# A skipped overflow branch moved to the third expert from the end, and one expert's rows turned a unit later

## The chip, the cores and the metric

The kernel runs on one core of a Trainium2 chip. The metric is the device time of one execution in microseconds (us). The engines that matter here are TensorE (PE), VectorE (DVE), ScalarE (ACT), GpSimd (POOL, which issues the gathers and scatters) and SyncE (SP, whose queue issues the loads of the weights).

## The reference, cut to what matters

Two encoder layers run over 512 tokens of width 1024. Each layer has four kinds of attention side by side, an output projection, and then a mixture of 16 experts (4 groups of 4). The change lies in the experts:

```python
def hier_moe(h, wg, bg, we, be, w_gate, w_up, w_down):
    ...
    expert_id = g_idx * EXPERTS_PER_GROUP + e_idx          # one group, two experts of it
    gate = jnp.sum(jax.nn.one_hot(expert_id, N_EXPERTS, dtype=jnp.float32) * (g_w * e_w)[..., None], axis=1)
    y = jnp.zeros_like(t)
    for e in range(N_EXPERTS):
        hid = jax.nn.silu(t @ w_gate[e]) * (t @ w_up[e])
        y = y + gate[:, e:e + 1].astype(t.dtype) * (hid @ w_down[e])
    return y.reshape(b, s, d)
```

All weights are float32. One expert has three matrices of 1024 x 512, 2 MB each.

## The kernel before

**Routing.** For each expert the kernel makes a list of up to `CAP` = 96 tokens that chose it. The rows of these tokens are gathered from DRAM (`gather`, L1477, an indirect DMA on POOL), turned on TensorE (`turn`, L1492) and multiplied with the expert's weights. The result is scaled (L1546, into the buffer `ye`) and added to the output in DRAM (`store`, L1547, an indirect DMA with addition).

**Overflow.** If some expert has more than 96 tokens, `overflow()` treats the rest in further rounds with loops over all experts. The number of rounds is read from `nrd` when the program runs; with these inputs it is 1, and the body below `with tc.If(rounds > 1)` (L1562) is skipped on every engine. The body loads weights with ScalarE's DMAs into the buffer `sg`, splits them into the buffer `ye`, and uses TensorE, DVE and POOL as well. `sg` is the same single buffer into which `silu` (L1511) writes for each expert.

**Precision.** Except for expert 0's gate and up products, which take the weights as loaded (L1504), each product is made of three matmuls on a high and a low part (`mm3`, L299). ScalarE makes the high part of each piece of weights (L155) and DVE the low part (L156). Up to six pieces are split ahead.

**Order.** `MOE_ORDER` interleaves the experts: 0 gate, 0 up, 1 gate, 0 down, 1 up, 2 gate, 1 down, 2 up, and so on to 15 up, 15 down. Each product is cut into four units of 512 KB of weights (a unit takes two of the eight 128-row blocks, or one of the four for down). In each unit the kernel issues TensorE's matmuls, splits further pieces as far as room allows, and does the small work that is tied to this unit: `hidden` (Silu's output times the up product, L1523) and `turn_hidden` (L1532) of the expert before, `turn` of the next expert, and the lists and the gather of a later one (L1465, L372). The order of the program is the order on each engine.

**Loads.** SyncE issues the weights in the same order (L195, L198) into some 26 buffers of 512 KB; a load is issued when a buffer's split is done. The loads run on eight lanes, each with a counter. Behind the expert weights of the first layer follow the weights of the second layer's projections.

**Around the change.** The branch stands behind expert 0's down product. Since its body uses `sg`, Silu of expert 1 cannot keep its place behind expert 1's gate product and is issued after the branch:

```python
                if m == 'g' and e != 1:
                    X[e].silu()
                elif m == 'd' and (last or e < NE - 1):
                    X[e].store()
                if (e, m) == (0, 'd'):

                    overflow()
                    X[1].silu()
```

The second place is `turn` of the next expert (`X[e + 1].turn()`), issued in unit 1 of the up product (units count from 0).

Of the kernel before, what the change touches and what calls it, by code (L numbers as in the profile page):

```python
# [23 lines left out]
NE = 16  # L24
# [33 lines left out]
def _bcast(ap, n=128):  # L58

    return bass.AP(tensor=ap.tensor, offset=ap.offset, ap=[[0, n]] + [list(d) for d in ap.ap])  # L60
# [3 lines left out]
def hybrid_encoder(ctx: ExitStack, tc: tile.TileContext, I: dict, out: bass.AP, depth=2, dbg=None):  # L64
# [289 lines left out]
    for layer in range(depth):  # L354
# [6 lines left out]
        X = {}  # L361
# [7 lines left out]
        def hots(e, oh):  # L369

            for t in range(NT):
                V.tensor_scalar(oh[:, t], iota, pos[:, t, e:e + 1], None, op0=OP.is_equal)  # L372
            return [oh[:, t] for t in range(NT)]
# [13 lines left out]
        with ExitStack() as c2:  # L387
# [475 lines left out]
            with ExitStack() as c3:  # L863
# [431 lines left out]
                g, d = list(range(32, 48)), list(range(48, 56))  # L1295
# [6 lines left out]
                for k, hd in enumerate(heads):  # L1302
                    first, m = place[k * NT], len(hd[2])
# [79 lines left out]
        with ExitStack() as c2:  # L1383
# [221 lines left out]
            def start(e):  # L1605
                rows, X[e] = X[e], Expert(xg[e % 2], X[e])
                if e > 1:
                    X[e].lists(lambda t: parts[:, t, e])
                else:
                    X[e].rows = rows  # L1610
                X[e].gather()
# [3 lines left out]
                          m=lambda: G.memset(xg[1], 0.0), S=lambda: start(1), K=weights,  # L1615
                          q=lambda: G.tensor_copy(parts[..., :2], tokb[:, :, None].to_broadcast([128, NT, NE, 2])))
            tail(TAIL[len(seq) + 5])
            for e, m in MOE_ORDER:
                us = wbase[layer, e, m][0]
                for i, u in enumerate(us):  # L1620
                    W.split(u + 1)
                    end = e == NE - 1 and m != 'g'
                    if m == 'd':
                        X[e].down(i, W.get(u))
                    elif end:
                        X[e].half(i, W.get(u))
                    else:
                        X[e].gu(m, i, W.get(u))
                    W.free(u + 1)
                    if end:  # L1630
                        if m == 'u' and i % 2:
                            X[e].hidden(i // 2)
                        if (m, i) == ('u', 2) or (m, i) == ('d', 0):
                            X[e].turn_hidden(m == 'd')
                    elif m == 'g' and i == 0 and e > 0:
                        X[e - 1].hidden()
                    upto = moe_units[-1] + 1
                    if end and m == 'd' and i > 1:
                        upto += W.RAW
                    W.split(min(u + (AHEAD if end else W.HL), upto), G if (m, i) in GS and not end else V)  # L1640
                    if m == 'g' and i == TH and e > 0:
                        X[e - 1].turn_hidden()
                    if m == 'u' and i == 1 and e + 1 < NE:
                        X[e + 1].turn()

                    for s, todo in FIRST if e < 2 else ((e + 3, (('u', 0), ('u', 2))),):
                        if e > 1:
                            todo = [(e,) + w for w in todo]
                        if (e, m, i) in todo and s < NE:
                            (start if (e, m, i) == todo[1] else listed)(s)  # L1650
                    if m == 'd' and e < 2:
                        if i == 0:
                            X[e].hots = hots(e, sm.tile([128, NT, CAP], BF, name="oh", bufs=2))
                        elif i == 2:
                            X[e].lists(lambda t: parts[:, t, e], rows=e == 0)
                    if m == 'g' and i == 0 and e == NE - 1 and not last:
                        (place, g1), = W.room(1)
                        g1 = g1.bitcast(FT)
                        SP.dma_start(g1, _bcast(I['norm1_g'][layer + 1]))
                    if m == 'u' and i == 0 and e == NE - 1 and not last:  # L1660

                        pt = ps.tile([128, NT, 128], FT, name="pto", tag="tr")
                        for t in range(NT):
                            PE.matmul(pt[:CAP, t], X[e].hots[t], identb, start=True, stop=True)
                        place = place[:, :512].rearrange("p (t c) -> p t c", t=NT)
                        A.activation(place[:CAP], pt[:CAP], AF.Copy)
                        V.tensor_copy(wlast, gate[:, :, NE - 1])
                if m == 'g' and e != 1:
                    X[e].silu()
                elif m == 'd' and (last or e < NE - 1):  # L1670
                    X[e].store()
                if (e, m) == (0, 'd'):

                    overflow()
                    X[1].silu()
                if m == 'd' and e == NE - 2 and not last:

                    for t in range(NT):
                        SP.dma_start(x_sb[:, t], stream[:, t])
# [91 lines left out]
```

## Time and profile before

| | |
|---|---|
| median of 3 runs | 1387.91 us (1387.12 to 1390.14) |
| profiled execution | 1392.77 us |
| its span, first to last instruction | 1391.0 us |
| TensorE busy | 1290.2 us (93%) |
| DVE busy | 1057.1 us (76%) |
| ScalarE busy | 857.8 us (62%) |
| POOL busy | 359.9 us (26%) |
| mean granted TensorE clock | 0.971 of full speed |
| moved by DMA | 278.44 MB, mean 200 GB/s |

The expert loops take about 380 to 700 us (first layer) and 1060 to 1391 us (second layer) of the span. Busy times are sums over stages with different limits; a busy TensorE includes the modelled ends of pipelined matmuls.

### The profile page before, as it was taken

To read this page: it belongs to the slowest core of one execution; us is meant where nothing else is said; L and a number is where in the kernel's file an instruction comes from. 1 tells how busy PE (TensorE), PEld (TensorE's weight loads), DVE (VectorE), ACT (ScalarE), POOL (GpSimd) and SP (SyncE) were. 2 spreads that over 40 slices of the span, in tenths; PEclk is the share of its full clock that TensorE was granted. 3 is DMA by queue.
4 is the path that set the end of the run, shared out by engine and by line. 5 is a ranking of instruction groups with operands and counts; after the bars stand their busy time and mean duration, and the time that the engine had idled before them with its cause. 6 is when DMAs were issued, how large, how long until landed. Compare 5 with 4: busy or idle time off the path is not lost. (4 is left out here: it accounts for less than half of the span.)

```text
span 1391.0 us, 21081 instructions
## 1 busy us (share of the span) xinstructions
PE 1290.2 (93%) x7182; PEld 1003.5 (72%) x7182; DVE 1057.1 (76%) x2073; ACT 857.8 (62%) x1419; POOL 359.9 (26%) x580
## 2 busy tenths in 40 slices
PE   9998899999986999999989998999998699999996
PEld 7776688888844666666778886888885366676674
DVE  5537866878575999999776587586966499999994
ACT  5343366664245888888744545676634378888884
POOL 3105333324411411111041161430344132111120
PEclk9999899999998999999999999999999899999998
DMA  8322341024597999999344223211176899999950
GB/s 230 100 78 63 133 138 41 15 67 168 217 382 264 352 366 362 366 365 329 109 118 125 78 75 79 69 37 31 48 307 239 303 312 358 370 365 366 367 201 13
DMA packets 100575, 278.44 MB, mean 200 GB/s; under 512 B 19466, under 2 KB 30522, under 8 KB 100457
## 3 DMA queue, kind: packets, MB, share of 16 engines
q1 hardware_dynamic: 89816, 249.00, 49.9%
q0 software_dynamic: 10352, 27.41, 7.9%
q8 instruction: 58, 0.95, 0.3%
q10 hardware_dynamic: 288, 0.59, 0.1%
q14 instruction: 61, 0.49, 0.1%
HBM read 264.34 MB, written 24.81 MB: 208 GB/s over the span
## 5 line engine op out<-in xcount | busy, mean ns | idle before, releaser
L156 DVE TENSOR_TENSOR lo<-raw,hi 128x1024 fp32r<-128x1024 f32 (+2 forms) x387 | 463.9, 1221 | 64.2 <-ACT hi L155 56.1
L155 ACT ACTIVATE hi<-raw 128x1024 fp32r<-128x1024 f32 (+1 forms) x393 | 405.4, 1051 | 99.6 <-PE pg L299 28.7
L299 PE MATMUL pm<-lo,hTh 128*128 128x512 f32 (+2 forms) x376 | 132.5, 352 | 5.9 <-DVE lo L156 5.9
L299 PE MATMUL pm<-hi,hTh 128*128 128x512 f32 (+2 forms) x376 | 134.3, 357 | 0.7 <-ACT hTh L155 0.5
L299 PE MATMUL pm<-hi,hTl 128*128 128x512 f32 (+2 forms) x376 | 132.0, 351 | 0.2
L299 PE MATMUL pd<-hi,hl 128*96 128x512 f32 x256 | 102.5, 400 | 4.5 <-DVE hl L156 2.8
L986 PE MATMUL pv<-v,pT 128*128 128x64 f32 x768 | 99.0, 272 | 6.5 <-DVE pT L974 2.7
L299 PE MATMUL pd<-lo,hh 128*96 128x512 f32 x256 | 101.2, 395 | 1.6 <-DVE lo L156 1.6
L986 PEld LDWEIGHTS pv<-v,pT 128*128 128x128 f32 x768 | 94.3, 193 | 10.8 <-DVE pT L974 5.0
L299 PE MATMUL pu<-hi,xh 128*96 128x512 f32 (+1 forms) x256 | 101.1, 395 | 0.6 <-PEq L1562 0.6
L299 PE MATMUL pd<-hi,hh 128*96 128x512 f32 x256 | 101.2, 395 | 0.0
L957 ACT ACTIVATE p<-p,m 128x512 f32<-128x512 f32 x96 | 68.7, 716 | 52.1 <-DVE m L939 51.7
L299 PE MATMUL pu<-hi,xl 128*96 128x512 f32 (+1 forms) x256 | 98.2, 384 | 0.0
L299 PE MATMUL pu<-lo,xh 128*96 128x512 f32 (+1 forms) x256 | 98.2, 384 | 0.0
L299 PE MATMUL pg<-hi,xh 128*96 128x512 f32 x240 | 96.8, 404 | 0.0
L299 PE MATMUL pg<-lo,xh 128*96 128x512 f32 x240 | 95.6, 398 | 0.0
L299 PE MATMUL pg<-hi,xl 128*96 128x512 f32 x240 | 95.3, 397 | 0.0
L299 PEld LDWEIGHTS pm<-lo,hTh 128*128 128x128 f32 x376 | 71.0, 189 | 16.0 <-DVE lo L156 8.0
L299 PEld LDWEIGHTS pm<-hi,hTh 128*128 128x128 f32 x376 | 70.9, 188 | 12.0 <-ACT hTh L155 1.0
L299 PEld LDWEIGHTS pm<-hi,hTl 128*128 128x128 f32 x376 | 71.0, 189 | 9.5 <-DVE hTl L156 0.9
L307 PE MATMUL ptr<-ident,p 128*128 128x128 f32 x512 | 77.3, 273 | 0.3 <-DVE pT L974 0.2
L307 PEld LDWEIGHTS ptr<-ident,p 128*128 128x128 f32 x512 | 63.8, 141 | 17.7 <-DVE pT L974 1.2
(389 smaller groups left out, 2772.5 us busy)
## 6 DMA issues: line engine op xcount, KB each, us to landing
raw<-in_expert_w_down_dram SPq DMA_DIRECT2D x118, 512.0 KB
raw<-in_expert_w_gate_dram SPq DMA_DIRECT2D x114, 512.0 KB
raw<-in_expert_w_up_dram SPq DMA_DIRECT2D x110, 512.0 KB
raw<-in_w_in_dram SPq DMA_DIRECT2D x32, 512.0 KB
raw<-in_w_out_dram SPq DMA_DIRECT2D x16, 512.0 KB
toep<-brep SPq DMA_DIRECT2D x16, 448.0 KB
x_sb<-in_expert_w_gate_dram SPq DMA_DIRECT2D x14, 512.0 KB
x_sb<-in_expert_w_up_dram SPq DMA_DIRECT2D x10, 512.0 KB
```

What stands on the lines that cost most here:

```text
L155: A.activation(hi, src, AF.Copy)
L156: E.tensor_tensor(lo, src, hi.bitcast(FT), op=OP.subtract)
L299: PE.matmul(pt, a, b, start=first and n == 0, stop=last and n == tot - 1)
L307: PE.transpose(pt[:c, i * 128:(i + 1) * 128], s, ident)
L957: A.activation(p, p, AF.Exp, bias=m, scale=-1.0, accum_out=s)
L986: PE.matmul(st['pv'][:, t], self.pT[:, k * 128:(k + 1) * 128], self.v(k), start=k == 0, stop=k == NT - 1)
```

## The change

The branch moves from behind expert 0's down product to behind expert 13's (`NE - 3`), and the Silu that is issued after it is no longer expert 1's but expert 14's (`NE - 2`). In the order of products, expert 14's gate stands before expert 13's down, and 14 up, 15 gate, 14 down, 15 up, 15 down follow. Besides, the rows of expert 1 are turned in unit 2 of expert 0's up product, and no longer in unit 1; for the other experts it stays unit 1.

```diff
-                    if m == 'u' and i == 1 and e + 1 < NE:
+                    if m == 'u' and i == (1 if e else 2) and e + 1 < NE:
                         X[e + 1].turn()
...
-                if m == 'g' and e != 1:
+                if m == 'g' and e != NE - 2:
                     X[e].silu()
                 elif m == 'd' and (last or e < NE - 1):
                     X[e].store()
-                if (e, m) == (0, 'd'):
+                if (e, m) == (NE - 3, 'd'):
 
                     overflow()
-                    X[1].silu()
+                    X[NE - 2].silu()
```

## Rows read from the trace of the kernel before

**Rows 1.** Windows: length, busy time of PE, PEld, DVE, ACT, POOL, PEclk, DMA share, GB/s.
```profile
410.00:424.00 14.00, 10.99 (x56) 7.34 (x54) 7.09 (x16) 5.50 (x7) 2.78 (x2) 1.00 1.03 351
424.00:440.00 16.00, 7.41 (x27) 5.16 (x27) 8.84 (x16) 7.99 (x10) 1.28 (x1) 0.68 0.52 166
...
500.00:520.00 20.00, 19.86 (x97) 13.91 (x96) 18.62 (x25) 16.55 (x20) 2.75 (x2) 1.00 1.01 366
...
1095.00:1112.00 17.00, 5.47 (x28) 3.47 (x26) 2.34 (x6) 3.54 (x5) 1.52 (x1) 0.82 0.65 219
1112.00:1130.00 18.00, 17.25 (x70) 12.00 (x71) 16.49 (x28) 12.42 (x16) 1.25 (x1) 0.79 0.84 275
```

**Rows 2.** Timeline of POOL: the stores of experts 0, 1, 2, then 0, 1.
```profile
417.65 1.52 POOL L1547 DMA_INDIRECT xd<-ye,ix  x1 [4.08 <-ACT ye L1546]
...
449.86 1.47 POOL L1547 DMA_INDIRECT xd<-ye,nrd  x1 [11.27 <-ACT ye L1546]
...
468.15 1.46 POOL L1547 DMA_INDIRECT xd<-ye,ix  x1 [3.40 <-DVE lo L156]
...
1097.15 1.52 POOL L1547 DMA_INDIRECT out_dram<-ye,ix  x1 [4.07 <-ACTq L1562]
...
1131.17 1.45 POOL L1547 DMA_INDIRECT out_dram<-ye,nrd  x1 [12.42 <-ACT ye L1546]
```

**Rows 3.** Timeline of PE: start, length, instruction, idle time before it, releaser.
```profile
432.59 0.78 PE L1465 MATMUL pli<-parts,oh 128*96 128x5 bf16 x4 [11.30 <-DVE oh L372]
...
1112.74 0.78 PE L1465 MATMUL pli<-parts,oh 128*96 128x5 bf16 x4 [11.98 <-DVE oh L372]
```

**Rows 4.** Timeline of ACT: the Silu of expert 1 in both layers.
```profile
429.56 0.59 ACT L1511 ACTIVATE sg<-pg 96x512 f32<-96x512 f32 x1 [12.19 <-SPq L1562]
...
1109.71 0.59 ACT L1511 ACTIVATE sg<-pg 96x512 f32<-96x512 f32 x1 [12.84 <-SPq L1562]
```

**Rows 5.** The line of the branch, 416 to 430 us: ns min/median/max, first and last start.
```profile
L1562 SPq EVENT_SEMAPHORE  x8: 17/17/17, 419.2 to 429.4; - x8
...
L1562 ACTq COMPARE_BRANCH  x1: 50/50/50, 416.7 to 416.7; - x1
...
L1562 POOLq INC_SWDGE_SEM  x1: 732/732/732, 418.2 to 418.2; - x1
...
L1562 ACTq EVENT_SEMAPHORE  x1: 17/17/17, 422.7 to 422.7; - x1
```

**Rows 6.** Waits of the load queue, 470:500, then 580:620: total us, times, longest.
```profile
SPq L198 <- DVE lo L156: 11.7, 12, 1.3
...
SPq L198 <- DMA raw<-in_expert_w_gate_dram: 9.3, 8, 2.1
```

**Rows 7.** Timeline of SP: issues of the last expert loads and the next ones.
```profile
652.28 2.42 SPq L195 DMA_DIRECT2D raw<-in_expert_w_down_dram  x4
673.86 1.51 SPq L195 DMA_DIRECT2D raw<-in_w_in_dram  x2
```

**Rows 8.** DMA in slices of 0.35 us, 655:669, then 1336:1350.
```profile
GB/s 249 228 293 222 275 304 298 334 357 386 398 433 456 398 386 363 316 281 257 199 152 105 94 35 0 0 0 0 0 0 0 0 0 0 0 0 0 0 0 0
...
GB/s 319 313 261 307 278 348 334 357 357 378 439 398 421 351 281 246 234 222 211 140 70 105 70 59 12 0 0 0 0 0 0 0 0 0 0 0 0 0 0 0
```

**Rows 9.** Timeline of ACT: expert 13's output in both layers.
```profile
667.19 1.24 ACT L1546 ACTIVATE ye<-pd,w 96x512 f32<-96x512 f32 x2
...
1348.48 1.24 ACT L1546 ACTIVATE ye<-pd,w 96x512 f32<-96x512 f32 x2
```

**Rows 10.** Timeline of PE around the turn of expert 1's rows.
```profile
388.95 3.60 PE L1504 MATMUL pu<-raw,xh 128*96 128x512 f32 x8
396.49 1.51 PE L1492 MATMUL ptg<-ident,xg 96*128 96x96 f32 x8 [3.94 <-DMA xg<-h2d,nrd]
397.80 6.01 PE L1504 MATMUL pu<-raw,xh 128*96 128x512 f32 x8
...
1076.24 1.51 PE L1492 MATMUL ptg<-ident,xg 96*128 96x96 f32 x8 [4.58 <-DMA xg<-h2d,nrd]
```

## The prediction

> **What bounds the kernel now.** I read the windows first, to see what each stage of the expert loop is limited by. In the steady stretch from 500 to 520 us TensorE is busy 19.86 of 20 us and the DMA engines are full at 366 GB/s: two resources at their limit at once, TensorE ahead by a hair [rows 1]. The stores give the beat: from one store to the next 18.29 us (449.86 to 468.15), which is what an expert costs [rows 2]. In both layers one stretch falls out of this, right behind expert 0: TensorE is busy 7.41 of 16 us from 424 to 440 and 5.47 of 17 us from 1095 to 1112, and there, alone in the loop, the DMA rate falls too, to 166 and 219 GB/s [rows 1].
>
> Then the timelines of TensorE and ScalarE, to see who waits for whom. TensorE stands still for 11.30 and 11.98 us, for a DVE operation that itself waits for work behind ScalarE [rows 3]. ScalarE stands still for 12.19 and 12.84 us in front of one instruction, the Silu of expert 1 (L1511), and what ends that wait is named L1562 on SyncE: the skipped branch [rows 4]. The line of the branch shows why. SyncE runs eight semaphore instructions there, spread from 419.2 to 429.4 us [rows 5]. At that time the load queue holds some eight weight loads of 512 KB; at the steady rate eight of them need 8 x 0.524 MB / 366 GB/s = 11.5 us, the length of the hold. I read this as follows: the branch's body issues loads into the buffer `sg`, so the empty path has to bring each load lane's counter up to date, and that can be done only when the lane's earlier load has landed. The skipped branch drains the load queue, and the Silu that follows writes `sg`.
>
> Last I looked at who waits in the load queue later on. From 470 to 500 us SyncE mainly waits for DVE to free a buffer (the loads are ahead); from 580 to 620 us it waits for earlier loads to land (the loads are the slower stream by then) [rows 6]. The last expert loads of layer 0 are issued from 652.28 to 654.7 us; the next layer's first loads come only at 673.86 [rows 7].
>
> **The change part by part.**
>
> *The early hold goes.* Silu of expert 1 returns to its place behind the gate product, and nothing of 0d waits for SyncE. Between the stores of experts 0 and 1 lie 449.86 - 417.65 = 32.21 us in the first layer and 1131.17 - 1097.15 = 34.02 in the second [rows 2]. Without the hold the same work (one expert) takes the beat of 18.29. Removed: 13.92 + 15.73 = 29.6 us. That is more than ScalarE's two waits (25.0) because TensorE comes out of them at a lower granted clock (0.68 in 424:440, 0.79 in 1112:1130 [rows 1]) and pays for that too. Nothing else is ready to fill that beat with a stall: the loads stand far ahead here, since SyncE waits for free buffers afterwards, not the other way round [rows 6].
>
> *Do the loads keep up?* They win less than the computation. In the hold they lost (366 - 166)/366 x 16 + (366 - 351)/366 x 14 = 9.3 us in layer 0, and 6.8 + 4.5 = 11.3 us in layer 1 (17 us at 219, 18 at 275) [rows 1]. The computation thus eats some 5 to 6 us of their lead per layer. That lead is large for the weights themselves: the last load has landed at about 663.4 us (the 24th slice of 0.35 us is the last that moves anything [rows 8]), when expert 13's output is not yet out (668.4 [rows 9]) and two experts are still to be computed. So the weights never run out, and I put nothing for them.
>
> *The late branch.* It now stands behind expert 13's down product, and Silu of expert 14 behind it. The order of work around it: ScalarE finishes expert 13's output at 667.19 + 1.24 = 668.4 and 1348.48 + 1.24 = 1349.7 us [rows 9]; the queue has run dry by 663.4 and 1336 + 25 x 0.35 = 1344.7 [rows 8]. Today the queue would be empty 5.0 us before ScalarE arrives. After the change ScalarE arrives earlier by 15.7 and 17.5 us (with the next item), the queue is empty earlier by 9.3 and 11.3, so ScalarE arrives 1.4 and 1.2 us too early and is held that long. No further loads stand in front of SyncE: the next layer's come 19 us behind the last expert load, after splits that belong to expert 14 [rows 7]. What is queued behind the Silu on ScalarE: the splits of expert 15's gate weights and rows, then DVE's halves of them, then TensorE. How much a hold costs TensorE can be read from the early one: 12.19 us cost 11.30 of standstill, 12.84 cost 11.98 [rows 3, 4], so hold less 0.9. For 1.3 us that is 0.4, and TensorE's own branch and a late split add a little: I take 1.0 a layer, 2.0 in all. Bounds: nothing (queue empty in time), and 12 us a layer, the early standstill again.
>
> [...] The row first: in layer 0 ScalarE takes the branch at 416.7 us, and its own semaphore instruction behind it comes only at 422.7 [rows 5]; SyncE's counters, later still, hid these 6.0 us. [...]
>
> *Expert 1's rows turned one unit later.* TensorE stands still for 3.94 and 4.58 us in front of these transposes (L1492), until the gather of the rows lands [rows 10]. The unit that now comes first is a quarter of expert 0's up product: four of the eight matmul records that take 3.60 us, so 1.80 us of work that moves into the idle time. The price is cover: the split of the turned rows on ScalarE and DVE, which expert 1's first product needs, then lies beside one unit of TensorE's work (1.8 us) in place of two. I take it as just enough. Gain 1.8 us a layer, 3.6 in all. Lower end 0 (the cover fails by as much); upper end 4.8 a layer, if TensorE, idle for 2.1 in place of 3.9 us, also keeps its clock: the eight records after the wait take 6.01 us in place of 3.60 and the transposes 1.51 in place of about 0.8 [rows 10]. I take the lower clock as it is today, being the nearest row.
>
> Sum against the profiled execution: 1392.8 - 29.6 - 3.6 + 2.0 = 1361.6 us (its span is 1391.0, 1.8 lie around it). The median of the runs is 4.9 below the profiled time, so 1356.7.
>
> **The rivals.**
>
> *The late hold is as real as the early one (0.20).* For it: the same eight lanes, the 6.0 us between ScalarE's branch and its semaphore [rows 5], and the computation arriving before the queue is empty. Against it: a queue that is nearly dry by then [rows 8]. With 4 to 12 us of standstill a layer in place of 1.0 the time is 1363 to 1379.
>
> *The weights bind (0.05).* If the loads' lead were gone, only their own gain of 9.3 + 11.3 = 20.6 us would come out: 1367. Against it: long after the hold SyncE still waits for DVE [rows 6].
>
> *The clock stays up at the early turn (0.12).* Up to 2 x 3.0 us more: 1351.
>
> *The end is later than today (0.04).* The branch also has to bring the store lanes up to date; if that made ScalarE wait for expert 13's scatter behind a full queue, the late hold would be 12.8 us plus the scatter's landing. The change loses from (29.6 + 3.6)/2 = 16.6 us of standstill a layer upward; at 20 it ends at 1388 + 2 x 3.4 = 1395. Against it: POOL's counter instruction in the branch took 0.73 us with a store just issued [rows 5].
>
> *The hold only moves (0.03).* The whole early price of 29.6 us, standstill and slow clock, is paid at the new place: 1388, or 1384 with the turn's 3.6.
>
> **How the numbers follow.** The forecast, 1353 to 1362, has 0.56; the likeliest value is 1357. The clock rival lies below it, the milder half of the late hold and the weights above. From 1349 to 1372 about 0.8 is held. What a measurement of this kernel can tell from no change is about 0.2%, 2.8 us. Faster by more: 0.56 + 0.20 + 0.05 + 0.12 = 0.93; same 0.03; slower 0.04.
>
> **What would show it.** Right: in the changed profile ScalarE has no wait for L1562 near 417 and 1085 us; the first two stores of each layer stand about 18.3 us apart; L1562 appears near 653 us and near 1318; SyncE's eight counters there lie within 3 us; TensorE has no gap over 2 us in the last three experts; and the wait in front of L1492 is about 2.1 and 2.8 us. Wrong: a ScalarE wait of over 5 us at the new place with a TensorE gap behind it, TensorE gaps with weight loads as releaser in experts 8 to 15, or DMA shares under 0.9 in the middle of the loop.

## The result and the profile after

The changed kernel takes 1365.65 us (median of 4 runs, 1364.60 to 1368.58); the kernel before, in the same rounds, takes 1388.89 (4 runs, 1387.12 to 1390.14). The ratio is 0.9837 with an interval of 0.9817 to 0.9857, so it is faster by 23.2 us. The sign and the range (1349 to 1372) hold. The forecast's own case, 1353 to 1362, does not: what came is the first rival, the late hold as real as the early one, though TensorE's standstill was shorter than that rival had it. The profiled execution took 1366.22 us, its span is 1364.1. Of the runs below one stands apart: of the four of the branch behind expert 14 one took 6083 us, for a reason that nothing here shows, and its ratio and the 1351.23 us given there leave it out.

The windows of the kernel after, first in the stretches of [rows 1] and then at the new place (length, busy time of PE, PEld, DVE, ACT, POOL, PEclk, DMA share, GB/s):

```profile
424.00:440.00 16.00, 16.00 (x84) 11.45 (x84) 14.78 (x26) 12.93 (x16) 2.77 (x2) 1.00 1.02 373
500.00:520.00 20.00, 19.86 (x97) 13.88 (x96) 18.56 (x25) 16.55 (x20) 2.74 (x2) 1.00 1.00 359
1095.00:1112.00 17.00, 16.64 (x83) 11.69 (x82) 15.64 (x24) 13.93 (x18) 2.76 (x2) 1.00 1.02 368
1112.00:1130.00 18.00, 17.53 (x87) 12.25 (x86) 16.59 (x23) 14.81 (x18) 3.06 (x2) 1.00 1.02 372
...
656.00:662.00 6.00, 5.06 (x11) 3.01 (x12) 6.00 (x8) 4.79 (x7) 0.00 (x0) 0.50 0.17 42
1325.00:1331.00 6.00, 5.23 (x12) 3.45 (x13) 6.00 (x8) 4.06 (x5) 0.00 (x0) 0.50 0.02 4
```

The hole behind expert 0 is gone in both layers: TensorE is busy 16.00 of 16 us where it was 7.41, at a granted clock of 1.00, and the loads run at 373 GB/s where they ran at 166 [rows 1]. A new one has opened late: in 656:662 and 1325:1331 TensorE is busy for 5.06 and 5.23 of 6 us, but at a granted clock of 0.50.

The stores on POOL's timeline (answering to [rows 2]) give the size of both:

```profile
411.01 1.52 POOL L1547 DMA_INDIRECT xd<-ye,ix  x1 [4.08 <-ACT ye L1546]
429.71 1.47 POOL L1547 DMA_INDIRECT xd<-ye,nrd  x1 [10.56 <-ACT ye L1546]
...
648.29 1.44 POOL L1547 DMA_INDIRECT xd<-ye,ix  x1 [16.19 <-DVEq L1562]
672.54 1.42 POOL L1547 DMA_INDIRECT xd<-ye,ix  x1 [22.81 <-ACT ye L1546]
...
1078.68 1.52 POOL L1547 DMA_INDIRECT out_dram<-ye,ix  x1 [4.07 <-ACT ye L1546]
1097.39 1.45 POOL L1547 DMA_INDIRECT out_dram<-ye,nrd  x1 [10.55 <-ACT ye L1546]
...
1316.42 1.43 POOL L1547 DMA_INDIRECT out_dram<-ye,ix  x1 [16.21 <-DVEq L1562]
1340.86 1.41 POOL L1547 DMA_INDIRECT out_dram<-ye,ix  x1 [23.00 <-ACT ye L1546]
```

From store 0 to store 1 it is now 18.70 and 18.71 us, for 32.21 and 34.02 before. From store 13 to store 14 it is 24.25 and 24.44, for 17.65 in both layers before:

```profile
668.71 1.44 POOL L1547 DMA_INDIRECT xd<-ye,ix  x1 [16.20 <-ACT ye L1546]
686.36 1.42 POOL L1547 DMA_INDIRECT xd<-ye,ix  x1 [16.21 <-ACT ye L1546]
...
1350.00 1.43 POOL L1547 DMA_INDIRECT out_dram<-ye,ix  x1 [16.20 <-ACT ye L1546]
1367.65 1.41 POOL L1547 DMA_INDIRECT out_dram<-ye,ix  x1 [16.22 <-ACT ye L1546]
```

Cut at such marks, the difference of the two spans (1364.1 - 1391.0 = -26.9) adds up:

| stretch | first layer | second layer |
|---|---|---|
| up to the list matmuls ahead of the loop (L1224), or from store 14 of the layer before | -3.5 | -0.5 |
| from there to store 0 | -3.1 | -4.2 |
| store 0 to store 1 | -13.5 | -15.3 |
| store 1 to store 13 | -0.3 | +0.2 |
| store 13 to store 14 | +6.6 | +6.8 |
| store 14 to the end | | -0.1 |

The 3.5 us ahead of the loop lie where nothing was changed; over all traces of this document, none of which changes anything there, these matmuls start anywhere from 373.6 to 379.6 us, and before has the latest. The profiled execution of before was itself 3.9 us above the median of the 4 runs, so the 3.5 are put down to that execution: without them the spans differ by 23.4 us, close to the 23.2 of the medians.

ScalarE's timeline at the new place (answering to [rows 4, 9]):

```profile
646.78 1.24 ACT L1546 ACTIVATE ye<-pd,w 96x512 f32<-96x512 f32 x2
653.66 0.59 ACT L1511 ACTIVATE sg<-pg 96x512 f32<-96x512 f32 x1 [5.65 <-SPq L1562]
...
1314.90 1.24 ACT L1546 ACTIVATE ye<-pd,w 96x512 f32<-96x512 f32 x2
1321.31 0.59 ACT L1511 ACTIVATE sg<-pg 96x512 f32<-96x512 f32 x1 [5.17 <-SPq L1562]
```

The branch's line, 640 to 655 us and then 1308 to 1325 (answering to [rows 5]: ns min/median/max, first and last start):

```profile
L1562 SPq EVENT_SEMAPHORE  x8: 17/17/17, 653.0 to 653.5; - x8
L1562 ACTq COMPARE_BRANCH  x1: 50/50/50, 647.7 to 647.7; - x1
L1562 ACTq EVENT_SEMAPHORE  x1: 17/17/17, 652.1 to 652.1; - x1
...
L1562 SPq EVENT_SEMAPHORE  x8: 17/17/17, 1314.3 to 1321.2; - x8
L1562 ACTq COMPARE_BRANCH  x1: 45/45/45, 1315.7 to 1315.7; - x1
L1562 ACTq EVENT_SEMAPHORE  x1: 17/17/17, 1316.2 to 1316.2; - x1
```

What the reader is to see: in both layers SyncE's last counter (653.5, 1321.2) ends the hold. In the second layer it is the only candidate, because ScalarE's own semaphore instruction comes 0.5 us behind its branch. In the first, ScalarE's own comes 4.4 us behind its branch, and would have held the Silu until 652.1 even without SyncE. Two different delays share the place. That SyncE itself waits for loads, and is not merely late, shows in the packets of the load queue: in the first layer the queue moves its last two in 652:653, just ahead of SyncE's counters, and in the second its last four in 1320:1321, just ahead of the last counter.

TensorE's timeline behind the holds, and around the turn (answering to [rows 3, 10]):

```profile
394.58 0.85 PE L1492 MATMUL ptg<-ident,xg 96*128 96x96 f32 x8 [0.84 <-DMA xg<-h2d,nrd]
395.26 1.88 PE L1504 MATMUL pu<-raw,xh 128*96 128x512 f32 x4
...
656.57 0.74 PE L299 MATMUL pg<-hi,xh 128*96 128x512 f32 x1 [2.84 <-ACT xh L155]
...
1324.22 0.48 PE L299 MATMUL pg<-hi,xh 128*96 128x512 f32 x1 [2.37 <-ACT xh L155]
```

TensorE works on through the first part of each hold and stands still for only 2.84 and 2.37 us, in front of expert 15's gate product, whose rows `xh` are made by ScalarE behind the held Silu. The slow matmuls cost as much again: in that stretch they start 0.43 us apart, ahead of the hold 0.23, and six microseconds at a granted clock of 0.50 are about three lost (an estimate from these numbers).

### The profile page after: what moved, and what is told of

It reads as the page before. It is cut to its first block, busy times and chain, and to the rows that moved or that the text cites. A ratio compares the mean times of both kernels' runs of the same rounds, so it can differ in the third digit from the quotient of the medians.

```text
span 1364.1 us, 21097 instructions
## 1 busy us (share of the span) xinstructions
PE 1286.9 (94%) x7182; PEld 1002.6 (74%) x7182; DVE 1058.3 (78%) x2073; ACT 857.3 (63%) x1419; POOL 337.0 (25%) x580
```

## The experiments

The theory after the result (A): the late hold is the early one over again. It is made by the loads in flight, whose counters the skipped body has to bring up to date, and its length is the distance between ScalarE's arrival and the load queue's running dry. The rival (B): each engine that jumps over the body comes back late by itself, wherever the branch stands, and loads have little to do with it. Every ratio is to the kernel before in the same rounds; the runs fall into four sets of rounds, in which that kernel's median is 1388.89 to 1390.51 us, so medians of different sets compare only roughly. A number in a kernel's name says behind which expert's down product its branch stands; the turn is the second part of the change.

**The branch left out altogether.** This kernel leaves out the overflow rounds. From the kernel after:

```diff
-                if m == 'g' and e != NE - 2:
+                if m == 'g':
...
-                if (e, m) == (NE - 3, 'd'):
-
-                    overflow()
-                    X[NE - 2].silu()
```

> The changed kernel without the overflow rounds at all (that part of the computation is left out), each Silu behind its own gate product. It gives the floor for any place of the branch. From the beats in the changed profile, expert 14's store comes 24.25 and 24.44 us after expert 13's in place of the 17.65 of before: 6.6 + 6.8 = 13.4 us. Theory (the skipped branch drains the load queue, and Silu, which writes the buffer that the branch's body loads into, waits for it): 1365.7 - 13.4 = 1352 us. Rival (the late loss is the end of the loop itself, where loads run out, and not the branch): 1365, with the same gap of 2 to 3 us on TensorE.

1353.36 us, ratio 0.9723 (0.9693 to 0.9753). Store 13 to 14 is 17.67 and 17.65 us, 0 to 1 is 18.72. So the branch at its new place costs some 12 us (12.3 by the medians, 13.4 by the stores), and this is the time that any other placement can be held against.

**The branch one expert later**, behind expert 14's down product, with Silu of expert 15 behind it. From the kernel after:

```diff
-                if m == 'g' and e != NE - 2:
+                if m == 'g' and e != NE - 1:
...
-                if (e, m) == (NE - 3, 'd'):
+                if (e, m) == (NE - 2, 'd'):
 
                     overflow()
-                    X[NE - 2].silu()
+                    X[NE - 1].silu()
```

> The branch one expert later still, behind expert 14's down product, with Silu of expert 15 behind it. Theory (drain): by then the last expert loads have landed, SyncE's eight counters follow each other within 1 us except for the three small first loads of the next layer in layer 0, ScalarE's wait at L1562 is under 1.5 us, and the time is 1352 to 1355. Rival (each taken branch costs ScalarE a fixed hold of some 5 us, for instance to fetch instructions): 5 us holds again and, since less work is left to cover them, 1365 or more.

1351.23 us, ratio 0.9720 (0.9682 to 0.9758): the whole cost is gone, as far as the intervals can tell, with the branch, its loads and its body as they were. The branch's line, first and last start over both layers, and the two Silus behind it:

```profile
L1562 SPq EVENT_SEMAPHORE  x16: 17/17/17, 657.7 to 1313.4; - x16
L1562 ACTq COMPARE_BRANCH  x2: 45/50/54, 662.7 to 1324.8; - x2
L1562 ACTq EVENT_SEMAPHORE  x2: 17/17/17, 663.1 to 1327.7; - x2
```

```profile
663.60 0.59 ACT L1511 ACTIVATE sg<-pg 96x512 f32<-96x512 f32 x1 [0.67 <-DVE wlast L1667]
...
1328.19 0.59 ACT L1511 ACTIVATE sg<-pg 96x512 f32<-96x512 f32 x1 [2.88 <-ACTq L1562]
```

In the second layer SyncE's last counter is through at 1313.4, and ScalarE comes to the branch at 1324.8; in the first the eight end at 659.6, ahead of ScalarE's 662.7. That is A's prediction. But ScalarE's own return took 2.9 us in the second layer, with no load left to wait for: B's delay exists, and here TensorE had no gap over 0.8 us behind it.

**The body's loads into a buffer of their own.** If the Silu waits because the body's loads write `sg`, it should be free when they write another buffer. The buffer is a small one (128 columns), so a block is loaded in four pieces. Edit of the kernel after:

```diff
-                    r = sm.tile([128, 512], FT, name="sg", bufs=1)
-                    A.dma_start(r, w)
                     hl = sm.tile([128, D], FR, name="ye", bufs=1)
-                    split(hl[:, :512], hl[:, 512:], r)
+                    for c in range(0, 512, 128):
+                        r = sm.tile([128, 128], FT, name="ow", bufs=1)
+                        A.dma_start(r, w[:, c:c + 128])
+                        split(hl[:, c:c + 128], hl[:, 512 + c:640 + c], r)
```

> The place of the changed kernel, but the skipped body loads its weights into a small buffer of its own (four loads of 128 columns) and no longer into the buffer that Silu writes. Theory (drain, and Silu held by the shared buffer): SyncE's eight counters still spread over some 5 us, but ScalarE has no wait named L1562 over 1 us, TensorE no gap, 1352 to 1354. Rival (the branch itself holds ScalarE, by fetching or by its own counter): ScalarE still waits 5 us and the time stays at 1365.

1365.83 us, ratio 0.9825 (0.9794 to 0.9855): nothing won, as the rival had it. The wait changed its owner, though:

```profile
653.74 0.59 ACT L1511 ACTIVATE sg<-pg 96x512 f32<-96x512 f32 x1 [4.98 <-DVEq L1563]
```

SyncE no longer ends it. DVE's and ScalarE's own semaphore instructions now come 5.3 and 4.2 us behind their branches (653.6 and 652.7, branches at 648.3 and 648.5), and 5.5 and 4.7 in the second layer. There the Silu starts at 1319.26, ahead of SyncE's last counter at 1319.7; in the first layer SyncE's last comes at 652.9, too near to tell. The edit took one hold away and, by making the body longer (four loads and splits for one), put the other in its place. The same edit with the branch at its old place and the turn kept:

> The branch at its old place behind expert 0's down product, the turn of expert 1's rows as changed, and the body's loads in a buffer of their own. Theory (drain): SyncE still drains the queue for some 11 us and the loads lose 6 to 10 us a layer, but nobody waits for SyncE; the loads' lead covers it, so 1352 to 1355, and then the old place was as good as the new one. Rival (it is the place that counts, since the drain starves the load stream): SyncE's pause is paid in weights that come late in experts 8 to 15, 1370 or more. Rival (the branch itself holds ScalarE): 12 us holds, 1381.

1369.00 us, ratio 0.9834 (0.9797 to 0.9870): neither 1352 to 1355 nor 12 us holds. Nor do weights come late: from store 1 to store 14 the first layer takes 236.5 us, as before the change.

```profile
416.97 0.59 ACT L1511 ACTIVATE sg<-pg 96x512 f32<-96x512 f32 x1 [5.70 <-DVEq L1563]
```

SyncE still counts its lanes off from 419.1 to 428.8 us, and nobody waits for it: the Silu is through at 417, where it stood until 429.56 [rows 4]. So SyncE's hold works through the buffer, as [rows 5] were read; with `sg` out of it the 12 us are gone, and a wait of 5.7 us (TensorE gaps of 3.84 and 3.69) is left, which is B's.

**Each part of the change alone.** The turn without the move, the only edit of the kernel before:

```diff
-                    if m == 'u' and i == 1 and e + 1 < NE:
+                    if m == 'u' and i == (1 if e else 2) and e + 1 < NE:
                         X[e + 1].turn()
```

> The kernel before with only the turn of expert 1's rows one unit later. By the prediction's term 1.8 us a layer, 3.6 in all: 1385 to 1387 against some 1390. From the changed profile (list of expert 0 to store of expert 0: 34.9 and 34.2 us in place of 38.0 and 38.4) 3.1 + 4.2 = 7.3 us: 1381 to 1383. Rival (the turn does nothing for the time): 1389 to 1390.

1391.13 us, ratio 1.0001 (0.9989 to 1.0013): worth nothing. The Silu, and TensorE's gap in both layers:

```profile
428.33 0.59 ACT L1511 ACTIVATE sg<-pg 96x512 f32<-96x512 f32 x1 [17.56 <-SPq L1562]
```

```profile
431.36 0.78 PE L1465 MATMUL pli<-parts,oh 128*96 128x5 bf16 x4 [16.67 <-DVE oh L372]
...
1111.09 0.78 PE L1465 MATMUL pli<-parts,oh 128*96 128x5 bf16 x4 [16.27 <-DVE oh L372]
```

ScalarE gets to the Silu earlier, SyncE's last counter comes at 428.2 as it did at 429.4 [rows 5], and the wait grows from 12.19 to 17.56 us. The loads set the end of the hold, and what the engines win ahead of it becomes waiting.

The move without the turn is the kernel after with that line put back (`i == 1`).

> The changed kernel with the turn put back to unit 1: the branch's move alone. By the beats in the changed profile 13.5 + 15.3 won early and 6.6 + 6.8 lost late: 15.4 us, so 1374 to 1375 against some 1390, and 7 us slower than the changed kernel if the turn is worth what the profile says; 3.6 slower if it is worth the predicted term.

1361.96 us, ratio 0.9802 (0.9783 to 0.9821). The expectation was missed by 12 us: expected 3.6 or 7 us slower than the changed kernel, the move alone is no slower than it. The late Silu and the stores around it:

```profile
651.65 0.59 ACT L1511 ACTIVATE sg<-pg 96x512 f32<-96x512 f32 x1 [2.70 <-PE ptg L1492]
```

```profile
649.22 1.44 POOL L1547 DMA_INDIRECT xd<-ye,ix  x1 [16.20 <-DVEq L1562]
669.76 1.42 POOL L1547 DMA_INDIRECT xd<-ye,ix  x1 [19.10 <-ACT ye L1546]
...
1318.34 1.43 POOL L1547 DMA_INDIRECT out_dram<-ye,ix  x1 [16.21 <-DVEq L1562]
1337.84 1.41 POOL L1547 DMA_INDIRECT out_dram<-ye,ix  x1 [18.08 <-ACT ye L1546]
```

ScalarE's waits are 2.70 and 1.68 us in place of 5.65 and 5.17, the beats 20.54 and 19.50 in place of 24.25 and 24.44. TensorE has no gap over 1.1 us there and keeps a granted clock of 1.00 in 652:664 and 1320:1332. Its turn waited for only 1.71 us in the first layer, where [rows 10] has 3.94, and TensorE kept its clock through that wait (the eight records behind it took 3.60 us). So the wait that the turn was to fill is not of a fixed size. Nor are the 2.70 us the loads' alone: SyncE's last counter comes at 650.6, ScalarE's own semaphore instruction at 651.2, 2.5 us behind its branch. In the second layer SyncE's last, at 1319.6, ends the wait.

**The old place, with nothing to load.** The branch behind expert 0 again, the turn kept, and every load of the body replaced by a memset (so this kernel and the next two leave out the overflow rounds):

```diff
                     r = sm.tile([128, 512], FT, name="sg", bufs=1)
-                    A.dma_start(r, w)
+                    V.memset(r, 0.0)
...
-                    A.dma_start(posd[0].rearrange("(t p) e -> p t e", p=128), pos)
-                    A.dma_start(posd[1].rearrange("(t p) e -> p t e", p=128), gate)
...
-                            for j in range(2):
-                                A.dma_start(pe_[:, j], posd[j, :, one].rearrange("(t p) o -> p (t o)", p=128))
+                            V.memset(pe_, 0.0)
```

> The branch at its old place, the turn as changed, and a skipped body of nearly the old length that has no load in it (its loads are replaced by memsets, so the overflow rounds are left out). Theory (two holds: SyncE's counters wait for loads that have to land, and apart from that an engine that jumps over a long body resumes late while the load queue is full): SyncE has no counters to bring up to date and the load stream goes on, yet ScalarE or DVE come back 5 to 6 us after their branch in some of the four cases: 1354 to 1368 by how many. Rival (the drain is all there is): every engine is back within 1 us, 1352 to 1354.

1354.21 us, ratio 0.9738 (0.9720 to 0.9755). The branch's line in both layers:

```profile
L1562 ACTq COMPARE_BRANCH  x2: 45/45/45, 407.1 to 1075.3; - x2
L1562 DVEq EVENT_SEMAPHORE  x2: 21/21/21, 407.6 to 1075.9; - x2
L1562 ACTq EVENT_SEMAPHORE  x2: 17/17/17, 407.8 to 1076.2; - x2
```

SyncE has no counters to run, the engines are back within 0.9 us while the load queue moves weights (6.68 MB in 404:425), and the old place costs next to nothing. That is the rival's case. The smallest body, a single memset in place of all of it, does not do better than the intervals can tell:

```diff
                 with tc.If(rounds > 1):
                     V.memset(off, 0.0)
-                    A.dma_start(posd[0].rearrange("(t p) e -> p t e", p=128), pos)
...
-                            x.store()
```

> The branch at its old place, the turn as changed, and a skipped body of a single memset on DVE (the overflow rounds are left out). Theory (two holds, both of the body: its loads and its length): no engine is late by more than 1 us and there is no gap on TensorE, 1352 to 1354, as without a branch. Rival (the condition and the join themselves cost): 1358 or more, with a gap behind the branch.

1352.79 us, ratio 0.9731 (0.9715 to 0.9746).

**A long body without loads** tells length from loads: the four-piece form of the own buffer, at the old place, with the turn, and memsets for all loads. Against the kernel without loads:

```diff
-                    r = sm.tile([128, 512], FT, name="sg", bufs=1)
-                    V.memset(r, 0.0)
                     hl = sm.tile([128, D], FR, name="ye", bufs=1)
-                    split(hl[:, :512], hl[:, 512:], r)
+                    for c in range(0, 512, 128):
+                        r = sm.tile([128, 128], FT, name="ow", bufs=1)
+                        V.memset(r, 0.0)
+                        split(hl[:, c:c + 128], hl[:, 512 + c:640 + c], r)
```

> The branch at its old place, the turn as changed, a skipped body as long as the one with its own buffer (four pieces a load) but with memsets in place of the loads, so the overflow rounds are left out. Theory (an engine that jumps over a long enough body resumes late): ScalarE and DVE come back 5 to 6 us after their branch as they did with the own buffer, TensorE has a gap of 3 to 4 us, 1362 to 1368. Rival (the length costs nothing; what held ScalarE and DVE with the own buffer came with its loads): back within 1 us, 1353 to 1355.

1364.91 us, ratio 0.9827 (0.9810 to 0.9844), some 11 us slower than the shorter body without loads (1354.21, in another set of rounds). The branch's line in both layers, and the Silu:

```profile
L1563 ACTq COMPARE_BRANCH  x2: 45/45/45, 405.8 to 1078.2; - x2
L1563 ACTq EVENT_SEMAPHORE  x2: 17/17/17, 412.0 to 1083.5; - x2
L1563 DVEq EVENT_SEMAPHORE  x2: 21/21/21, 412.0 to 1084.2; - x2
```

```profile
412.16 0.59 ACT L1511 ACTIVATE sg<-pg 96x512 f32<-96x512 f32 x1 [5.73 <-DVEq L1563]
```

ScalarE is back 6.2 and 5.3 us behind its branch, with no load in the body at all, and the stores 0 and 1 stand 25.12 and 25.02 us apart. B is real too, and no load is needed for it: of two bodies without loads, ScalarE and DVE come back late behind the longer one (ScalarE after 6.2 and 5.3 us) and at once behind the shorter (0.7 and 0.9).

**The changed kernel and the best one once more**, in one set of rounds, with the turn of the best one undone as the third.

> The changed kernel once more, beside the next ones on one chip. Theory (the end of a hold is set by the loads, so what the turn wins ahead of the branch is lost at the branch, and TensorE's standstill there lowers its clock as well): ratio 0.983 to 0.985, some 3 us slower than the move alone had (0.980). Rival (that difference was chance): 0.979 to 0.981.

1364.99 us, ratio 0.9819 (0.9795 to 0.9842); stores 13 to 14 24.38 and 24.67 us apart. The ratio lies between the two cases, and its interval overlaps that of the move alone (0.9783 to 0.9821): that the turn makes the changed kernel slower is not shown; that it makes it no faster is.

> The branch behind expert 14's down product, with the turn as changed, once more: no hold at either place. 1351 to 1354, ratio 0.972 to 0.974.

1354.50 us, ratio 0.9751 (0.9733 to 0.9769): about 10 us faster than the changed kernel, now in a direct comparison.

The branch behind expert 14 without the turn (`i == 1` again):

> The same with the turn put back to unit 1. Here no hold stands behind the turn and the computation sets the time, so the turn's own worth shows. By the predicted term of 1.8 us a layer it is 3.6 us slower than with the turn, 1355 to 1358. Rival (the turn wins nothing even without a hold behind it, since the gather's landing and not TensorE's order sets the start of expert 1): 1351 to 1354.

1357.15 us, ratio 0.9769 (0.9749 to 0.9788). It is 2.65 us slower than with the turn, and the intervals overlap. The traces agree with the median: from the list matmuls (L1224) to store 14 the two kernels with the branch behind expert 14 and the turn take 288.4 to 289.2 us in their four passages, this one 290.3 and 290.8. By these few executions the turn is worth about 1.7 us a layer where no hold follows, near the predicted 1.8; the intervals alone would also allow nothing.

## Why the prediction was right, and where its sizes were off

**The signs.** Of the signs named, ScalarE's wait is gone at the old place, the first stores stand 18.7 us apart, and L1562 appears at the new place; SyncE's counters lie within 0.5 us there in the first layer, but spread over 6.9 in the second. But the sign of being wrong came too, in both layers: ScalarE waits over 5 us at the new place, with a TensorE gap behind it. That the time still fell in the range is partly luck: the range had been made wide enough for that rival, and another miss, ahead of store 0, went the other way.

**The early hold: right.** The mechanism (the empty path counts off lanes whose loads are under way, and the Silu waits through `sg`) stood up to four kernels: without loads (three of them) and with loads into another buffer, the wait for SyncE is gone at the old place. Measured 13.5 + 15.3 = 28.8 us for 29.6; the beat that comes in its place is 18.70, not 18.29.

**The late branch: the mis-sized term.** It was put at 1.0 us a layer and measured 6.6 and 6.8. That is the rival "the late hold is as real", priced there at 1363 to 1379. Of the miss of 7.8 us in the spans (31.2 worked out, 23.4 found) it is 11.4; the early hold adds 0.8, while the way up to store 0 gave 3.7 more than worked out (7.3 for 3.6) and the other stretches 0.7. Two steps of the working failed.

The first is the length of the hold. It was worked out as 1.4 us from a margin of 5.0 us, less what ScalarE gains on the queue. In the first layer ScalarE arrives at 646.78 + 1.24 = 648.0, which is 20.4 us earlier than before (3.5 from ahead of the loop, 3.1 up to store 0, 13.5 from the hold, 0.3 behind it) and not 15.7; SyncE's counters are through at 653.5, only 9.9 earlier than the 663.4 at which the queue was empty before. So 20.4 - 9.9 - 5.0 = 5.5 us, the hold that is seen. In the second layer 33.6 us for ScalarE, 23.5 for the loads (1344.7 to 1321.2) and the same 5.0 give 5.1, and 5.17 is measured. Measured from the list matmuls of each layer, so without what comes from ahead of it, ScalarE gained 16.9 and 19.3 us where 15.7 and 17.5 were worked out, and the loads, up to SyncE's last counter, 6.4 and 9.2 where 9.3 and 11.3 were: both terms missed toward a longer hold. Why the loads gained less is not shown. The difference of two large numbers was taken as exact to a microsecond; its right form was a range from nothing to some 6 us.

The second is "hold less 0.9" for TensorE. That rule was read from holds of 12 us. In holds of 5.65 and 5.17 TensorE stands still for only 2.84 and 2.37, but its clock then falls to 0.50 over 6 us, about three more lost, with smaller waits of 0.37 and 0.83 for DVE behind: 6.2 us in both layers, of the 6.6 and 6.8. In the move alone a wait of 2.70 left the clock at 1.00 and cost 2.9 us.

**The return of the engines: named, and not taken into the sum.** ScalarE's 6.0 us between branch and semaphore [rows 5] were noted. In the first layer of the changed kernel the same gap is 4.4 us and lies beside SyncE's counters, which end 1.4 us later, so there it adds nothing; in the second it is 0.5.

**The turn: about its size, and lost at the hold.** It was put at 1.8 us a layer, from one execution. From the list matmuls to store 0 the three kernels without it take 35.2 to 38.4 us, and the eleven with it 33.1 to 34.9 in all passages but one (36.6). So it does win ahead of the hold, but not a fixed amount, because the wait that it fills varies: in [rows 10] it is 3.94 and 4.58 us, in the move alone 1.71 and 3.78. Against the move alone the changed kernel wins 0.84 us up to store 0 in the first layer and 4.05 in the second. The rival in which the clock stays up came true as a mechanism: behind the new wait of 0.84 us the four records took 1.88 us, where eight took 6.01 before [rows 10], and in the second layer the changed kernel has no wait there at all. What failed is the step from there to the end of the kernel: where a hold follows, its end is set by the loads, and the gain becomes waiting. Alone, the turn measured 1.0001. In the full change the waits at the late branch are longer by 2.95 and 3.49 us than in the move alone. In the second layer that is the turn's gain: counted from the list matmuls ScalarE comes 4.1 us earlier, SyncE's last counter only 0.6. In the first ScalarE comes 1.1 us earlier and SyncE's last counter 2.8 later; why the loads end later in that execution is not shown.

**The end later, the hold only moved: neither came.** POOL's counter instruction at the new place took 1.22 and 1.27 us and nothing waited for it; of the early price of 28.8 us, 13.4 came back.

**The weights never bind: right.** From store 1 to store 13 the changed kernel is within 0.3 us of the one before.

## What to carry to other kernels

In this kernel a skipped branch was not free (at its new place it cost some 12 us against none), and its price lay in its body (with a single memset in the body, at the old place, the time is 1352.79 us). The body issues loads, and the empty path waited for the loads that were already under way (ScalarE stood 12.19 and 12.84 us before the change, 5.65 and 5.17 after it); so compare the time at which the queue runs dry with the time at which the engines arrive, and put the branch behind both. Here one expert further on gave another 10 us or more (1354.50 for 1364.99 us in the same rounds, a ratio that the intervals cannot tell from no branch at all) for a change of three numbers. And before counting a small gain, ask what sets the end of the next hold: if it is the loads, whatever the engines win ahead of it turns into waiting, as here, where the turn alone made ScalarE's wait in the first layer 17.56 us in place of 12.19 and the kernel no faster (ratio 1.0001).

## What the runs showed of the hardware that was not expected

ScalarE can come back late from a skipped body by itself. Behind the branch of the four-piece body, ScalarE's own semaphore instruction came after 4.2 to 6.5 us in all six passages (three kernels, two layers), with loads in the body or without. Behind the shorter body without loads it came after 0.7 and 0.9. Behind the body of the kernel itself it differs from layer to layer: 6.0 and 0.9 before, 4.4 and 0.5 after, 0.4 and 2.9 with the branch behind expert 14. This is no chance of one execution: the kernel with the turn alone repeats the first pair (6.1 and 0.9), the second execution of the changed kernel the second (4.4 and 0.5), and the two further ones with the branch behind expert 14 the third (0.5 and 2.6 to 2.7).

With it goes one thing in the traces, packets on a queue that the profile names instruction, q14, between ScalarE's branch and its semaphore instruction:

| kernel | ScalarE back after, us (layers 1, 2) | q14 packets meanwhile |
|---|---|---|
| before | 6.0, 0.9 | 3, 0 |
| after | 4.4, 0.5 | 4, 0 |
| branch behind expert 14 | 0.4, 2.9 | 0, 2 |
| shorter body without loads | 0.7, 0.9 | 0, 0 |
| long body without loads | 6.2, 5.3 | 2, 3 |

Over all thirteen traces with a branch the two never part: the 14 late returns (2.5 us and more) have two to four such packets each, the 12 returns within 0.9 us have none.

```profile
q14 instruction: 2, 0.02, 0.6%
```

That is the DMA view of the long body without loads, 405 to 413 us. What the packets carry, and for which engine, the traces do not say, and that the engine waits for them is not shown; the two come together, no more. That a body's length alone decides is ruled out by the kernel's own body, which is late in one layer (6.0 us) and not in the other (0.9).

A standstill of TensorE can cost its own length again in clock (2.84 us and then, by the estimate above, about three), but its length alone does not tell whether it will. Gaps of 2.84 and 2.37 us in the changed kernel were followed by 6 us at 0.50 of full speed, while behind the gaps of 0.84 and 1.07 us of the move alone it stayed at 1.00. It also stayed at 1.00 behind longer gaps elsewhere: 2.91 us in front of the turn in the kernel without loads (395:405) and 2.94 in the kernel with the turn alone (1075:1085); the four records behind each took 1.88 us. What tells these apart is not shown here.
